# First operands of the last weights' products loaded and split inside the last gate and up block, residual loads placed later, the last form bank by bank

## The chip, the cores and the metric

The kernel runs on one core of one Trainium2 chip. The metric is the device time of one launch in microseconds, the median of several runs; before the change it was 1640.43 us (3 runs, 1640.39 to 1641.12). Engines: TensorE (PE, its weight loads PEld), VectorE (DVE), ScalarE (ACT), GpSimd (POOL) and SyncE (SP), which issues all transfers of the stage looked at here.

## The reference, cut to what matters

One decoder layer on 1024 tokens of width 1024: retention and differential attention side by side, a cross attention to 256 memory tokens, and a gated feed forward net with 2816 hidden columns. The change touches only the end:

```
h = rms_norm(x, norm_ffn[l])
x = x + (jax.nn.silu(h @ w_gate[l]) * (h @ w_up[l])) @ w_down[l]
```

All is float32.

## The kernel before, in words

**Float32 by halves.** Each operand is split into a high part (`sc.copy` on ScalarE rounds it to fp32r) and a low part (`low`, a subtraction on VectorE). `mm3` (line 131) makes a product of three matmuls: high with high, high with low, low with high.

**Gate and up** (lines 1187 to 1226). The hidden columns go in 22 blocks of 128, j = 0 to 21. Both matrix products of a block, gate and up, are done together by a scheme of seven products instead of eight: `Forms.form(f)` makes the seven sums or differences of weight quarters (f = 1, 2, 5, 6, 3, 7, 4) and splits them, `GU.prod(f)` is 12 matmuls (4 row blocks by 3) into one of three PSUM banks x, y, z, and `GU.after(f)` reads a bank when its sum is complete. The banks accumulate over several products, so a later product of the same bank waits until VectorE or ScalarE has read it. `after(7)` adds bank x into `U` on VectorE and then multiplies on GpSimd; `after(4)` multiplies on VectorE. The loop is rotated: in step j the last two products of block j (7 and 4) stand between the first five of block j + 1. In the last step, j = 21, there is no next block: products 7 and 4 stand alone with their reads between them.

**Down.** The product with `w_down` uses seven products as well. The seven forms of its left operand are made by `g_forms` (two blocks j make one pair p, 11 pairs) and stored in DRAM as `gF`; those of the weights by `w_forms`, stored in DRAM as `wT`; some quarters are used as they are. Then the loop in lines 1241 to 1265 goes over the forms f = 1, 2, 6, 5, 7, 3, 4 and, inside, over the pairs p = 0 to 10. Each (f, p) loads 128 x 512 of the left and 128 x 512 of the right operand (256 KB each, two issues on SP) into a stage tile `ds`, casts it (`dh`), subtracts (`dl`), and does 4 x 3 matmuls of 128 x 512 into four PSUM banks X or Y. After a form its four banks are added on VectorE to the residual tiles `res`, and finished quarters go to the output.

**Residual.** The eight tiles `res` (512 KB each) are loaded from DRAM, where an earlier stage has stored them. They lie in the four buffers of tag B (two tiles in each), which before hold the gate and up weights of the last two blocks (`gu`) and the two halves of form 4 of the activations (`B4`, read by product 4 of every block).

**Buffers.** Stage tiles of tag st (function `raw`): 3. Of tag t4: 6, used in the loop for `G`, for sums of weights, and for `gSa` and `gSb`, the sums of `g_forms`. Of tag xn (`xnp_tile`): 2, used for two of the weight sums. Split operands (tag w): 9, two for each (f, p).

**What sets the order.** A planner orders the instructions of each engine before the launch; on the chip every engine then goes through its list in that order, waiting on semaphores. An instruction issued while `pin[0]` is set stays behind everything that the program has traced on its engine before; this holds for the whole gate and up loop. TensorE's instructions always keep program order. Other instructions may move up to where the planner thinks them ready, which the loads of the down loop did.

Of the kernel before, what the change touches and what calls it, by code (L numbers as in the profile page):

```python
# [9 lines left out]
F32 = mybir.dt.float32  # L10
F32R = mybir.dt.float32r
# [5 lines left out]
P = 128  # L17
S = 1024
D = 1024
NT = 8  # L20
# [3 lines left out]
NH = HID // P  # L24
EPS = 1e-6
MAGIC = 0x5F3759DF
NP = NH // 2
# [3 lines left out]
U_RET, U_DIF, U_OUT, U_KV, U_XQ, U_XO, U_GU, U_DN = 0, 16, 28, 36, 52, 60, 68, 112  # L31
# [6 lines left out]
def body(ctx, tc, a, out):  # L38
# [18 lines left out]
    ve, sc, gp, sp = (Engine(e) for e in (nc.vector, nc.scalar, nc.gpsimd, nc.sync))  # L57
# [15 lines left out]
    up = ctx.enter_context(tc.tile_pool(name="up", bufs=NW))  # L73
# [8 lines left out]
    def t4(name, dt=F32):  # L82
        return tp4.tile([P, 1024], dt, tag="t4", name=name)
# [10 lines left out]
    def s2(name):  # L94
        return ps_s.tile([P, 1024], F32, tag="S", name=name)
# [8 lines left out]
    def low(eng, dst, src, hi):  # L104

        eng.tensor_tensor(out=dst, in0=src, in1=hi.bitcast(F32), op=ALU.subtract)

    def raw(name):
        return stp.tile([P, 1024], F32, tag="st", name=name)
# [21 lines left out]
    def mm3(ps, pairs, start=True, stop=True, **kw):  # L131

        n = len(pairs)
        for i, ((lh, ll), (rh, rl)) in enumerate(pairs):
            pe.matmul(ps, lh, rh, start=start and i == 0, stop=False, **kw)
            pe.matmul(ps, lh, rl, start=False, stop=False, **kw)
            pe.matmul(ps, ll, rh, start=False, stop=stop and i == n - 1, **kw)
# [631 lines left out]
    bp = p2.enter_context(tc.tile_pool(name="bp", bufs=1))  # L769
# [99 lines left out]
    res_d = [drp.tile([P, D], F32, tag=f"res{t}", name=f"res_d{t}") for t in range(NT)]  # L869
# [159 lines left out]
    def add(eng, dst, x, y):  # L1029
        eng.tensor_tensor(out=dst, in0=x, in1=y, op=ALU.add)  # L1030

    def sub(eng, dst, x, y):
        eng.tensor_tensor(out=dst, in0=x, in1=y, op=ALU.subtract)
# [39 lines left out]
    wd, wT = {}, {}  # L1073

    def w_load(p):
        wd[p] = [raw(f"wd{p}_{i}") for i in range(2)]
        for i in range(2):
            sp.dma_start(wd[p][i], a["w"][U_DN + 2 * p + i])

    def w_forms(p):  # L1080

        r = wd.pop(p)
        B11, B12, B21, B22 = r[0][:, 0:512], r[0][:, 512:1024], r[1][:, 0:512], r[1][:, 512:1024]
        sub(ve, B11, B12, B11)
        sub(ve, B12, B22, B12)
        sub(ve, B22, B22, B11)
        sub(ve, B21, B21, B22)
        wT[p] = drp.tile([2, P, 1024], F32, tag=f"wT{p}", name=f"wT_d{p}")
        for i in range(2):
            sp.dma_start(wT[p][i], r[i])  # L1090

    gF, Gs = {}, {}

    def g_forms(p):

        g1, g2 = Gs.pop(2 * p), Gs.pop(2 * p + 1)
        A11, A21, A12, A22 = g1[:, 0:512], g1[:, 512:1024], g2[:, 0:512], g2[:, 512:1024]
        x, y = t4(f"gSa{p}"), t4(f"gSb{p}")
        d = drp.tile([4, P, 1024], F32, tag=f"gF{p}", name=f"gF_d{p}")
        sp.dma_start(d[0][:, 0:512], A11)  # L1100
        sp.dma_start(d[1], g2)
        add(ve, x[:, 0:512], A21, A22)
        sub(ve, x[:, 512:1024], x[:, 0:512], A11)
        sub(ve, y[:, 0:512], A11, A21)
        sub(ve, y[:, 512:1024], A12, x[:, 512:1024])
        sp.dma_start(d[2], x)
        sp.dma_start(d[3], y)
        gF[p] = d

    class GU:  # L1110
# [37 lines left out]
        def go(self, f, c=slice(0, 512)):  # L1148
            self.prod(f, c)
            if f not in (1, 6):  # L1150
                self.after(f, c)

    c0, c1, call_ = slice(0, 256), slice(256, 512), slice(0, 512)
    f0 = Forms(0)
    f0.form(1, gp)
# [30 lines left out]
    pin[0] = True  # L1186
    for j in range(NH):
        n, c = None, c1 if j == 0 else call_
        if j % 2 == 0:
            w_load(j // 2)  # L1190
        if j + 1 < NH:
            n = GU(j + 1, fn)
            fm = Forms(j + 2) if j + 2 < NH else None
            n.prod(1)
            fn.form(5)
        o.prod(7, c)
        if n:
            fn.form(6)
            fn.form(3)
        o.after(7, c)  # L1200
        if n:
            n.prod(2)
            fn.form(7)
            n.after(2)
        o.prod(4, c)
        if n and fm:
            fm.form(1)
        o.after(4, c)
        if n:
            n.prod(5)  # L1210
            if fm:
                fm.form(2)
            n.after(5)
            n.prod(6)
            fn.form(4)
        if j % 2 == 0:
            w_forms(j // 2)
        if n:
            n.prod(3)
        if j % 2:  # L1220
            g_forms(j // 2)
        if n:
            n.after(3)
            fn = fm
        o = n
    pin[0] = False

    res = [bp.tile([P, 2, D], F32, tag="B", bufs=4, name=f"res{t}") for t in range(4)]
    res = [res[t // 2][:, t % 2] for t in range(NT)]
    for t in range(NT):  # L1230
        sp.dma_start(res[t], res_d[t])
    xs_ = [s2(f"dx{i}") for i in range(2)]
    X = [xs_[i // 2][:, 512 * (i % 2):512 * (i % 2) + 512] for i in range(4)]
    Y = [(mm, ms)[i // 2](f"dy{i}") for i in range(4)]
    gsrc = {1: (0, 0), 2: (1, 0), 4: (1, 1), 5: (2, 0), 6: (2, 1), 7: (3, 0), 3: (3, 1)}
    wsrc = {5: (0, 0), 7: (0, 1), 4: (1, 0), 6: (1, 1)}

    outs = {1: [(X, 0, 0)], 2: [(Y, 0, 0, 1)], 6: [(X, 0, 1)], 5: [(Y, 1, 1)], 7: [(X, 1, 1, 1)],
            3: [(Y, 0, 1, 1)], 4: [(X, 1, 0, 1)]}
    h5_ = lambda i: slice(512 * i, 512 * i + 512)  # L1240
    for f in (1, 2, 6, 5, 7, 3, 4):
        bank = Y if f in (2, 5, 3) else X
        for p in range(NP):
            s_ = raw(f"ds{f}_{p}")
            d, x = gsrc[f]
            sp.dma_start(s_[:, 0:512], gF[p][d][:, h5_(x)])
            if f in wsrc:
                d, x = wsrc[f]
                sp.dma_start(s_[:, 512:1024], wT[p][d][:, h5_(x)])
            else:  # L1250
                sp.dma_start(s_[:, 512:1024], a["w"][U_DN + 2 * p + (f > 1)][:, h5_(f == 3)])
            hi, lo = (up.tile([P, 1024], F32R, tag="w", name=f"d{x}{f}_{p}") for x in "hl")
            sc.copy(hi, s_)
            low(ve, lo, s_, hi)
            for i in range(4):
                sl = slice(P * i, P * i + P)
                mm3(bank[i], [((hi[:, sl], lo[:, sl]), (hi[:, 512:1024], lo[:, 512:1024]))],
                    start=p == 0 and f in (1, 2, 5), stop=p == NP - 1, skip_group_check=f not in (1, 2, 5))
        for b_, e, c, *last in outs[f]:
            for i in range(4):  # L1260
                t = 2 * i + e
                dst = res[t][:, h5_(c)]
                add(ve, dst, b_[i], dst)
                if last:
                    sp.dma_start(out[t][:, h5_(c)], dst)
    p2.close()


# [67 lines left out]
def build(arrays):  # L1336
    nc = bacc.Bacc("TRN2", target_bir_lowering=False, num_devices=1, dynamic_dma_scratch_size=1024)
    aps = {k: nc.dram_tensor(f"in_{k}_dram", v.shape, mybir.dt.from_np(v.dtype), kind="ExternalInput").ap()
           for k, v in arrays.items()}
    out = nc.dram_tensor("out_0_dram", (NT, P, D), F32, kind="ExternalOutput").ap()  # L1340
    with tile.TileContext(nc) as tc:
        with ExitStack() as ctx:
            body(ctx, tc, aps, out)
    return nc
# [10 lines left out]
```

## Time and profile before

| | |
|---|---|
| median of 3 runs | 1640.43 us |
| profiled execution, its own time | 1642.59 us |
| its span | 1640.8 us |
| TensorE busy | 1547.2 us, 94% |
| VectorE, ScalarE, GpSimd busy | 64%, 38%, 17% |
| chain that ended last | PE 75%, DVE 16%, ACT 3%, DMA 3% |
| mean granted TensorE clock | 0.982 |
| a residual load, a store of gF (gSa, gSb, second G), a store of wT | 512 KB |
| one operand pair of the down products | 2 x 256 KB |

Times are us from the start of the span. Busy shares are averages over all stages; what is read below is the stretch from the last gate and up block (from 1379 us) through the first down form (1417.7 to 1456.7) to the end. In a timeline row, the bracket at the end says how long the engine stood idle before the instruction and what released it. In a windows row the granted clock stands as a share of full speed (1.00 is 2.4 GHz, 0.50 is 1.2 GHz).

### The profile page before, as it was taken

What the parts mean: (1) busy time and instruction counts of PE and PEld (TensorE: products, weight loads), DVE (VectorE), ACT (ScalarE), POOL (GpSimd) and SP (SyncE); (2) the same over time, 40 slices, a digit from 0 to 9 for tenths busy, and PEclk for the clock granted to TensorE, in tenths of its full rate; (3) what the DMA queues carried; (4) which work ended last, traced back from release to release, by engine and by line L of the source; (5) the groups of instructions that cost most, each with busy time, mean ns of one, the idle gap of its engine ahead of it and who ended that gap; (6) DMA issues with size and microseconds to landing.
All of it is one profiled execution on the core that took longest, in us unless ns stands there. A gap on an engine that the chain in (4) does not pass through costs nothing.

```text
span 1640.8 us, 23170 instructions
## 1 busy us (share of the span) xinstructions
PE 1547.2 (94%) x8712; PEld 1321.6 (81%) x8712; DVE 1046.6 (64%) x2578; ACT 616.3 (38%) x1187; POOL 283.1 (17%) x238
## 2 busy tenths in 40 slices
PE   5899899999999989999999979999999999899998
PEld 5778878878877978799899858788888888688887
DVE  8864873873876543756666886666666666455554
ACT  4442442442444731333223353333333333243332
POOL 4323222222212331102112230010000000000000
PEclk9899999999999999999999989999999999999999
DMA  8201110110102562101101122444444444766564
GB/s 286 71 27 39 34 51 27 44 52 26 39 27 97 187 217 84 46 1 39 39 27 39 65 103 84 148 148 147 148 161 147 168 163 171 255 215 219 195 218 154
DMA packets 68079, 180.82 MB, mean 110 GB/s; under 512 B 7296, under 2 KB 12800, under 8 KB 67968
## 3 DMA queue, kind: packets, MB, share of 16 engines
q1 hardware_dynamic: 66960, 178.81, 30.8%
q8 instruction: 68, 1.11, 0.3%
q10 hardware_dynamic: 1008, 0.55, 0.1%
q14 instruction: 43, 0.35, 0.1%
HBM read 135.55 MB, written 43.78 MB: 109 GB/s over the span
## 4 chain that ended last, share of the span: by engine, by line
PE 75%; DVE 16%; ACT 3%; DMA 3%; issue 1%; POOL 1%; SPq 0%; ACTq 0%; DVEq 0%; POOLq 0%
PE x L64 14%; PE g_r L64 8%; PE z L64 7%; PE dx L64 7%; PE dy L64 5%; PE wo L64 5%; PE xo L64 5%; PE xq L64 4%; PE y L64 3%; PE kv L64 3%; PE q L64 2%; PE av L64 2%; DVE dsm L52 2%; DVE rw_d L52 2%; DVE nmx L52 1%
## 5 line engine op out<-in xcount | busy, mean ns | idle before, releaser
L64 PE MATMUL g_r<-uh_r,xT 128*128 128x512 f32 x512 | 178.2, 406 | 0.0
L52 DVE TENSOR_TENSOR dl<-ds,dh 128x1024 fp32r<-128x1024 f32 x77 | 94.2, 1224 | 98.0 <-PE dy L64 36.6
L52 ACT CAST dh<-ds 128x1024 fp32r<-128x1024 f32 x77 | 81.2, 1054 | 133.1 <-DMA ds<-in_w_dram 41.5
L64 PE MATMUL kv<-uh_d,xT 128*128 128x256 f32 x512 | 112.4, 302 | 6.2 <-DVE dql L52 6.2
L64 PE MATMUL x<-Bh,f 128*128 128x512 f32 (+1 forms) x368 | 114.6, 383 | 1.5 <-DVE G L52 1.4
L64 PEld LDWEIGHTS g_r<-uh_r,xT 128*128 128x128 f32 x512 | 96.4, 188 | 22.3 <-issue 2.5
L52 DVE TENSOR_TENSOR f<-s,f 128x512 fp32r<-128x512 f32 x86 | 65.0, 756 | 62.8 <-ACT f L52 62.8
L52 POOL TENSOR_TENSOR G<-G,U 128x512 f32<-128x512 f32 (+1 forms) x23 | 35.6, 1549 | 399.2 <-DVE U L52 381.3
L64 PE MATMUL g_r<-ul_r,xT 128*128 128x512 f32 x256 | 100.6, 393 | 0.0
L64 PEld LDWEIGHTS kv<-uh_d,xT 128*128 128x128 f32 x512 | 88.3, 200 | 8.7 <-DVE dql L52 6.4
L64 PE MATMUL xq<-hT,uh_xq 128*128 128x256 f32 x512 | 94.3, 286 | 0.0
L52 ACT CAST f<-s 128x512 fp32r<-128x512 f32 x88 | 54.6, 620 | 104.2 <-DVE s L52 102.5
L64 PE MATMUL xo<-uh_xo,xoT 128*128 128x512 f32 x256 | 90.2, 412 | 2.1 <-DVE B6l L52 1.6
L52 ACT ACTIVATE p<-s,nmx,dsm 128x128 f32<-128x128 f32 (+7 forms) x64 | 53.2, 832 | 98.6 <-DVE nmx L52 95.3
L64 PEld LDWEIGHTS x<-Bh,f 128*128 128x128 f32 x368 | 69.2, 191 | 15.2 <-DVE G L52 2.1
L64 PEld LDWEIGHTS xq<-hT,uh_xq 128*128 128x128 f32 x512 | 81.0, 195 | 0.0
L64 PE MATMUL kv<-ul_d,xT 128*128 128x256 f32 x256 | 74.8, 292 | 1.9 <-DVE ul_d L52 1.9
L52 DVE TENSOR_TENSOR f<-gu,f 128x512 fp32r<-128x512 f32 x63 | 43.4, 689 | 49.2 <-ACT f L52 49.2
L64 PE MATMUL dx<-dh 128*128 128x512 f32 x176 | 69.6, 396 | 5.2 <-ACT dh L52 5.2
L64 PE MATMUL xq<-hT,ul_xq 128*128 128x256 f32 x256 | 73.1, 286 | 0.0
L52 DVE TENSOR_TENSOR G<-x,G 128x512 f32<-128x512 f32 (+1 forms) x69 | 45.7, 662 | 41.9 <-ACT G L52 38.5
L64 PE MATMUL x<-Bl,f 128*128 128x512 f32 (+1 forms) x184 | 70.3, 382 | 0.0
(325 smaller groups left out, 4247.1 us busy)
## 6 DMA issues: line engine op xcount, KB each, us to landing
gu<-in_w_dram SPq DMA_DIRECT2D x21, 1024.0 KB, 6.0
ds<-gF_d SPq DMA_DIRECT2D x77, 256.0 KB, 2.9
wd<-in_w_dram SPq DMA_DIRECT2D x22, 512.0 KB, 5.6
wT_d<-wd SPq DMA_DIRECT2D x22, 512.0 KB, 3.0
ds<-wT_d SPq DMA_DIRECT2D x44, 256.0 KB, 3.4
ds<-in_w_dram SPq DMA_DIRECT2D x33, 256.0 KB, 3.3
st_r<-in_w_dram SPq DMA_DIRECT2D x16, 512.0 KB, 3.3
st_kv<-in_w_dram SPq DMA_DIRECT2D x16, 512.0 KB, 3.3
```

The source lines that it names most:

```text
L52: r = f(*args, **kw)
L64: return tc.keep_in_program_order(nc.tensor.matmul(*args, **kw))
```

## The change

A function `d_load` issues the two loads of a pair (f, p) into a given kind of tile, and `d_cast` casts and subtracts. In the last step of the gate and up loop, with the order pinned, the pairs p = 0, 1, 2 of form 1 are loaded at its start (into the two xn tiles and one stage tile) and split at three places: before `after(7)`, before `after(4)`, and at the end of the step behind `g_forms`. In the down loop the residual loads stand just before the pair p = 4 of the first form instead of before everything. Stage tiles alternate: odd pairs use tag st, even pairs tag t4. In the last form (f = 4) the products of the last three pairs are done bank by bank, each bank followed by its add and output.

```
+    def d_load(f, p, stage):
+        ds[f, p] = s_ = stage(f"ds{f}_{p}")
+        d, x = gsrc[f]
+        sp.dma_start(s_[:, 0:512], gF[p][d][:, h5_(x)])
...
+    def d_cast(f, p):
+        s_ = ds.pop((f, p))
+        hi, lo = du[f, p] = [up.tile([P, 1024], F32R, tag="w", name=f"d{x}{f}_{p}") for x in "hl"]
+        sc.copy(hi, s_)
+        low(ve, lo, s_, hi)
...
     for j in range(NH):
         n, c = None, c1 if j == 0 else call_
+        if j == NH - 1:
+            for p in range(3):
+                d_load(1, p, raw if p == 2 else xnp_tile)
...
+        else:
+            d_cast(1, 0)
         o.after(7, c)
...
         o.prod(4, c)
-        if n and fm:
+        if not n:
+            d_cast(1, 1)
+        elif fm:
             fm.form(1)
         o.after(4, c)
...
         if j % 2:
             g_forms(j // 2)
+        if not n:
+            d_cast(1, 2)
...
-    for t in range(NT):
-        sp.dma_start(res[t], res_d[t])
...
+    for f in d_order:
         for p in range(NP):
...
+            if f == d_order[0] and p == 4:
+                res2 = [bp.tile([P, 2, D], F32, tag="B", bufs=4, name=f"res{t}") for t in range(4)]
+                res = [res2[t // 2][:, t % 2] for t in range(NT)]
+                for t in range(NT):
+                    sp.dma_start(res[t], res_d[t])
+            if (f, p) not in du:
+                d_load(f, p, raw if p % 2 else t4)
+                d_cast(f, p)
+            if f != d_order[-1] or p < NP - 3:
+                for i in range(4):
+                    d_prod(f, p, i)
+        if f == d_order[-1]:
             for i in range(4):
+                for p in range(NP - 3, NP):
+                    d_prod(f, p, i)
+                d_out(f, i)
```

`d_prod(f, p, i)` is the `mm3` of bank i, `d_out(f, i)` the adds and outputs of bank i, both as they stood in the loop.

## Rows read from the trace of the kernel before

**Rows 1.** The chain of waits that ended last: start us, us, what

```profile
1414.04 0.70 DVE U L52
...
1414.88 3.00 PE x L64 x12
...
1417.88 5.47 PE dx L64 x24
...
1425.31 7.50 DMA ds<-in_w_dram
...
1432.91 1.05 ACT dh L52
...
1433.99 1.23 DVE dl L52
...
1435.27 21.41 PE dx L64 x83
...
1636.23 0.69 DVE res L52
```

**Rows 2.** Timeline of TensorE: start us, us, engine, instruction, idle time before

```profile
954.44 0.63 PE L68 MATMUL bt<-ident,bs 128*128 128x128 f32 x4 [2.63 <-DVE ry_f L52]
...
1413.61 0.39 PE L64 MATMUL x<-Bh,f 128*128 128x512 f32 x1
...
1434.01 0.79 PE L64 MATMUL dx<-dh 128*128 128x512 f32 x1 [5.17 <-ACT dh L52]
```

**Rows 3.** Windows: length us, PE busy (instructions), granted clock, DMA share, GB/s

```profile
955.00:955.75 0.75, 0.72 (x5) 0.80 0.00 0
...
958.75:959.50 0.75, 0.75 (x8) 0.92 0.00 0
...
1433.00:1433.50 0.50, 0.00 (x0) 0.82 0.84 324
...
1440.00:1440.50 0.50, 0.50 (x3) 0.85 1.03 295
```

**Rows 4.** Timeline of the SP queue: start us, us of issuing, transfer

```profile
1386.50 0.32 SPq L52 DMA_DIRECT2D res<-res_d  x1
...
1389.40 1.82 SPq L52 DMA_DIRECT2D wd<-in_w_dram  x2
...
1391.26 0.45 SPq L52 DMA_DIRECT2D res<-res_d  x1
...
1391.76 0.48 SPq L52 DMA_DIRECT2D ds<-gF_d  x1
...
1406.00 0.79 SPq L52 DMA_DIRECT2D res<-res_d  x2
...
1417.68 0.32 SPq L52 DMA_DIRECT2D res<-res_d  x1
...
1422.17 0.32 SPq L52 DMA_DIRECT2D gF_d<-gSb  x1
...
1422.54 2.20 SPq L52 DMA_DIRECT2D res<-res_d  x3
...
1424.84 0.42 SPq L52 DMA_DIRECT2D ds<-gF_d  x1
```

**Rows 5.** Timeline of VectorE: start us, us, engine, instruction, idle time before

```profile
1405.29 0.69 DVE L52 TENSOR_TENSOR f<-gu,f 128x512 fp32r<-128x512 f32 x1 [3.27 <-ACT f L52]
...
1419.12 1.22 DVE L52 TENSOR_TENSOR dl<-ds,dh 128x1024 fp32r<-128x1024 f32 x1
...
1634.87 2.65 DVE L52 TENSOR_TENSOR res<-dx,res 128x512 f32<-128x512 f32 x4 [8.24 <-PE dx L64]
```

**Rows 6.** DMA rate from 1390 to 1440 us in 40 slices

```profile
GB/s 403 256 302 328 403 392 113 13 0 0 0 0 0 56 387 380 413 390 197 329 402 375 243 300 328 374 410 275 383 252 397 365 323 398 324 48 21 252 138 192
```

**Rows 7.** Timeline of ScalarE: start us, us, engine, instruction, idle time before

```profile
1416.52 1.05 ACT L52 CAST dh<-ds 128x1024 fp32r<-128x1024 f32 x1 [4.92 <-DMA ds<-in_w_dram]
```

**Rows 8.** The output transfers: duration ns min/median/max, first and last start us

```profile
L52 SPq DMA_DIRECT2D out_dram<-res x16: 332/338/430, 1485.8 to 1637.5; - x16
```

More of the change, by code (lines that the diff above doesn't have):

```diff
@@ L1151, in go @@
                 self.after(f, c)
+    gsrc = {1: (0, 0), 2: (1, 0), 4: (1, 1), 5: (2, 0), 6: (2, 1), 7: (3, 0), 3: (3, 1)}
+    wsrc = {5: (0, 0), 7: (0, 1), 4: (1, 0), 6: (1, 1)}
+    d_order = (1, 2, 6, 5, 7, 3, 4)
+    ds, du = {}, {}
+    h5_ = lambda i: slice(512 * i, 512 * i + 512)
+    def d_load(f, p, stage):
+        ds[f, p] = s_ = stage(f"ds{f}_{p}")
+        d, x = gsrc[f]
+        sp.dma_start(s_[:, 0:512], gF[p][d][:, h5_(x)])
+        if f in wsrc:
+            d, x = wsrc[f]
+            sp.dma_start(s_[:, 512:1024], wT[p][d][:, h5_(x)])
+        else:
+            sp.dma_start(s_[:, 512:1024], a["w"][U_DN + 2 * p + (f > 1)][:, h5_(f == 3)])
+    def d_cast(f, p):
[3 more added lines that the diff above has]
+        low(ve, lo, s_, hi)
     c0, c1, call_ = slice(0, 256), slice(256, 512), slice(0, 512)
@@ L1199, in body @@
             fn.form(3)
+        else:
+            d_cast(1, 0)
         o.after(7, c)
@@ L1226, in body @@
     pin[0] = False
-    res = [bp.tile([P, 2, D], F32, tag="B", bufs=4, name=f"res{t}") for t in range(4)]
-    res = [res[t // 2][:, t % 2] for t in range(NT)]
-    for t in range(NT):
-        sp.dma_start(res[t], res_d[t])
+    res = []
     xs_ = [s2(f"dx{i}") for i in range(2)]
@@ L1234, in body, with d_prod @@
     Y = [(mm, ms)[i // 2](f"dy{i}") for i in range(4)]
-    gsrc = {1: (0, 0), 2: (1, 0), 4: (1, 1), 5: (2, 0), 6: (2, 1), 7: (3, 0), 3: (3, 1)}
-    wsrc = {5: (0, 0), 7: (0, 1), 4: (1, 0), 6: (1, 1)}
     outs = {1: [(X, 0, 0)], 2: [(Y, 0, 0, 1)], 6: [(X, 0, 1)], 5: [(Y, 1, 1)], 7: [(X, 1, 1, 1)],
             3: [(Y, 0, 1, 1)], 4: [(X, 1, 0, 1)]}
-    h5_ = lambda i: slice(512 * i, 512 * i + 512)
-    for f in (1, 2, 6, 5, 7, 3, 4):
-        bank = Y if f in (2, 5, 3) else X
-        for p in range(NP):
[L1244 to L1254, printed above, removed]
+    def d_prod(f, p, i):
+        hi, lo = du[f, p]
+        sl = slice(P * i, P * i + P)
+        mm3((Y if f in (2, 5, 3) else X)[i], [((hi[:, sl], lo[:, sl]), (hi[:, 512:1024], lo[:, 512:1024]))],
+            start=p == 0 and f in (1, 2, 5), stop=p == NP - 1, skip_group_check=f not in (1, 2, 5))
@@ new lines, in d_out @@
+    def d_out(f, i):
+        for b_, e, c, *last in outs[f]:
+            t = 2 * i + e
+            dst = res[t][:, h5_(c)]
+            add(ve, dst, b_[i], dst)
+            if last:
+                sp.dma_start(out[t][:, h5_(c)], dst)
+    for f in d_order:
+        for p in range(NP):
+            if f == d_order[0] and p == 4:
[10 more added lines that the diff above has]
+        if f == d_order[-1]:
@@ L1255, in body @@
             for i in range(4):
[L1256 to L1259, printed above, removed]
+                for p in range(NP - 3, NP):
+                    d_prod(f, p, i)
+                d_out(f, i)
+        else:
             for i in range(4):
[L1261 to L1265, printed above, removed]
+                d_out(f, i)
```

## The prediction, made before the change was run

> **What bounds the kernel now.** I read the chain of waits first, over its last 240 us [rows 1]. Up to 1409 us it is TensorE alone, block after block; from 1435.27 us on it is TensorE alone again. Between them it leaves TensorE three times. Twice VectorE must read a PSUM bank before the next product may add to it; the second time it is the add into U (0.70 us), which ends 0.14 us before the last gate/up product starts at 1414.88. Then the first form of the down products begins and runs out of operands: a load (7.50 us of DMA), a cast on ScalarE (1.05) and the subtraction on VectorE (1.23) stand in the chain before TensorE goes on. That is the fifth operand pair, p = 4: 4 pairs of 12 products each were ready, the fifth was not.
>
> The timeline of TensorE shows the price [rows 2]: 5.17 us of idle time before the product at 1434.01, then a wait for the low part until 1435.27 [rows 1]. The windows with the granted clock show the second half of it [rows 3]: the clock falls from full to 0.5 (from 2.4 to 1.2 GHz) in the window at 1433.0 and is full again only in the window at 1440.0. Altogether: 7 forms x 132 products at 29.92/132 = 0.227 us would take 209.4 us from 1417.7; they took until 1636.2, so 9.0 us are lost, all in this form. The two waits for VectorE's reads of a bank are short beside that.
>
> Why is p = 4 late? The issue order of the SP queue tells it [rows 4]. Once the last gate/up product has ended (1417.88), SP issues one residual load, three stores of gF, three more residual loads (2.20 us of issuing), and only at 1424.84 the load of p = 4. The bytes in between are seven transfers of 512 KB; with p = 4's own 512 KB, 4.19 MB. It was cast at 1432.91.
>
> **Two rules of order, read from the same rows.** The planner gives buffers of one tag away in program order: of the three stage buffers two held the weights loaded at 1389.40, the third had been free for the whole loop, and yet the first down load came at 1391.76, right after them. Among what is ready it takes what stands earlier in the program: weights (1389.40) before the second residual load (1391.26) that had been ready since 1386.50, and that before the down load. I assume that both rules hold in the changed kernel.
>
> **The change, part by part.**
>
> *First pair, loaded inside the last block.* The loads of p = 0 to 2 are pinned on SP behind the two stores of wT. Those wait for four subtractions after the split of the last form at 1405.29 [rows 5]; with pitches of 0.6 us the first store goes at 1407.2, the second at 1408.4, the load of p = 0 at 1408.9 to 1409.3. (Before, it was issued at 1391.76 and its data lay there in time. So this edit makes it 17 us later.) Ahead of it in the queue: the residual load of 1406.00 and both stores. Whether one or two residual loads go ahead is a choice: the same pattern one block earlier (a buffer free, two VectorE operations, a store) let one residual load through at 1386.50 and the next only at 1391.26, behind what stood earlier in the program [rows 4]. I take one: 4 x 0.524 = 2.10 MB. The DMA rate by slices of 1.25 us [rows 6] is 56 GB/s to 1407.5 and then 387, 380, 413, 390: 2.03 MB by 1412.5, so 2.10 MB at 1412.7. From bytes to cast is 1.0 us: the first load behind the stores (2.88 MB by the same sum, reached at 1415.5) let the cast start at 1416.52 [rows 7]. So p = 0 can be cast at 1413.7.
>
> Here lies a new wait. The cast and the subtraction of p = 0 are pinned ahead of the add into U. Behind the cast on ScalarE nothing urgent queues; behind the subtraction on VectorE queues the add into U, and for that TensorE waits. 1413.7 + 1.05 + 1.23 + 0.70 + 0.14 and 0.05 of gaps = 1416.85 against 1414.88: **+2.0 us** (with two residual loads ahead +3.3; if the load were early, 0).
>
> *Its clock.* TensorE then idles from 1414.0 (the last matmul before, at 1413.61, and its 0.39) [rows 2] to 1416.85, 2.9 us. The nearest row is the idle time of 2.63 us before 954.44 [rows 2]: the clock was down from about 955.2 to 958.9 [rows 3], some 3.5 us at half speed, which cost 1.7 us. I take **+1.7**; bounds 0 and 3.3 (the 6.7 us of low clock after the 5.17 us, halved). The product starts at 1416.85, so most of it falls inside it, and its end moves from 1417.88 to 1421.6.
>
> *p = 1, 2, 3.* Loads of p = 1 and 2 follow at 1.35 us each (0.524 MB at 0.39), their casts are done before TensorE asks for them at 2.7 us apart; the subtraction of p = 2 stands behind the last multiplication and the four form sums (0.7 + 4 x 0.6 us after the product's end) and is ready 4.4 us after it, needed after 5.4. p = 3 takes the buffer of the first stored weight. No cost: bounds 0 and 1, hidden by what comes next. The store of gF's first quarter moves behind six issues; its reader is p = 10 of this form, 27 us later.
>
> *Residual loads later; p = 4 in a t4 buffer.* Residual loads now stand in the program behind p = 3, still ahead of p = 4. Four of them need the two buffers of B4, free when the last product ends, as at 1417.68. And p = 4 now takes a t4 buffer: by the first rule not before gSb of the last block has its own, which is the third of the four form sums after that product. By then four residual loads are ready and stand earlier. So the order of rows 4 repeats: residual, three stores, three residuals, p = 4. **The stall stays.** What changes is a little: the subtraction of 1.22 us that lay between the form sums at 1419.12 [rows 5] is ahead of the product now, so gSb's store and all behind it go 1.2 us earlier. Before, from the product's end to p = 4's second product: 1435.27 - 1417.88 = 17.4. I take 17.4 - 1.2 = 16.2. Upper end 17.4 (as before). Lower end 15.3: 4.19 MB at 390 GB/s, the best sustained rate of rows 6, 10.75 us, plus 1.2 from issue to first bytes, 1.0, 1.05, 1.23 and 0.1 of gaps. So p = 4's second product starts at 1421.6 + 16.2 = 1437.8, **+2.5** against 1435.27, in which the +2.0, +1.7 and -1.2 are contained.
>
> What the rate is worth: between 1418.75 and 1431.0 the slices give 342 GB/s. The Trainium skill (DMA: Bandwidth & Descriptors, Specifications) states about 358 GB/s as the HBM limit of a core; by that these 4.19 MB would take 11.7 us, an estimate, in place of 12.3, and the sum would be 0.6 us lower. The trace's slices of 413 GB/s lie above that limit, so I go by the slices.
>
> *Clock after p = 4.* Idle 1421.6 + 10.9 = 1432.5 to 1436.5, 4.0 us, against 5.17: same fall, 0. Lower bound -2.4 (12 products at 0.427 in place of 0.227, if it stayed up).
>
> *Forms 2 to 7.* Nine stage buffers in place of three. TensorE has no idle time there (the chain is TensorE without a break from 1435.27 on), so nothing to gain: 0.
>
> *Last form bank by bank.* The last three pairs run bank after bank, so banks end 9 products (2.0 us) apart instead of 3 (0.7). Before, four adds of 0.69 on VectorE queue from 1634.87 on for 2.65 us [rows 5], and the last output is issued at 1637.5 [rows 8]; the last product had released VectorE at 1636.23 [rows 1]. The last add can start then, some 0.6 us sooner than as fourth in that queue: **-0.6**. Bounds 0 and -1.2 (an emptier DMA queue). Pairs 8 to 10 must be split before bank 0 ends; the last subtraction was done 8.24 us before 1634.87, at 1626.6; TensorE asks for it at 1636.2 less 30 products of 0.227, 1629.4: covered by 2.8 us.
>
> **Sum.** +2.5 + 0 - 0.6 = +1.9 us on the profiled execution (span 1640.8, its time 1642.59, 2.2 us above the median of the runs). Taken to the median 1640.43: **1642.3**, I write 1642. Own range: 1639.5 to 1644.5, from +3.3 for two residual loads, the clock's 0 to 3.3, and 15.3 to 17.4.
>
> **The rivals.**
> *A residual load more in front of the first pair* (slower). Place: the SP queue at 1406. Both residual loads went there before (the row of 1406.00 has x2) [rows 4]. Then p = 0 lands at 1415.0, U is 3.3 us late, TensorE idles 4.2 us and the low clock costs up to 3.3 as after the 5.17 us: 1.9 + 1.3 + 1.6 = +4.8, 1645.2. It decides from a landing later than about 1414.5. Against: the pattern of 1386.50.
> *p = 4 goes ahead of the residual loads.* Then the 9.0 us go, the late U stays (+3.7), the tail gives 0.6: -5.9, 1634.5. For: that the loads are in another place in the program. Against: both rules of order.
> *All covers hold*, first pair in time too: -9.0 - 0.6 = -9.6, 1630.8. Against: the issue at 1409 behind 2 MB.
> *The change does next to nothing*: U in time, p = 4 as late as before: -1.2 - 0.6 = -1.8, 1638.6. It would take a landing by 1411.7.
>
> **How the numbers follow.** Forecast 0.58, one more residual load 0.15, p = 4 early 0.15, all covers 0.06, next to nothing 0.06. What can be told from no change here is 0.2%, 3.3 us: below 1637.1 faster, above 1643.7 slower. Faster: 0.15 + 0.06 + 0.03 (a forecast with every bound low) = 0.24. Slower: 0.14 of the second case and 0.06 of the forecast's upper end = 0.20. Same 0.56. The range reaches down to the p = 4 case and up to the second: 1634 to 1645.5.
>
> **What would show it.** Right: the first gate/up product after U starts about 1416.9, VectorE's add into U waiting for the subtraction of dl; in the SP queue p = 4 behind four residual loads; an idle time of 3 to 5 us in the first down form again, with a clock of 0.5 behind it; the last add alone. Wrong: the first down form without idle time, p = 4 issued before the residual loads, or the last gate/up product starting at 1414.9 as before.

## The result and the profile after

The changed kernel takes 1650.26 us (median of 5 runs, 1646.46 to 1652.14) against 1640.39 us before (5 runs on the same chip, 1637.25 to 1641.12): ratio 1.0062, interval [1.0045, 1.008]. It is slower, and 8.3 us above the forecast of 1642.0. Two more measurements gave 1.0044 [1.003, 1.0059] and 1.0038 [1.0024, 1.0051].

The profiled execution has a span of 1650.3 us, 9.5 us more than before. Not all of it belongs to the change. ScalarE reads bank z into G once in every gate and up block. The first and the last of these reads, in the trace of before and then in that of after:

```profile
985.28 0.37 ACT L52 COPY G<-z 128x256 f32<-128x256 f32 x1 [1.78 <-PE z L64]
...
1409.62 0.59 ACT L52 COPY G<-z 128x512 f32<-128x512 f32 x1 [3.42 <-PE z L64]
```

```profile
989.85 0.37 ACT L52 COPY G<-z 128x256 f32<-128x256 f32 x1 [1.77 <-PE z L64]
...
1413.97 0.59 ACT L52 COPY G<-z 128x512 f32<-128x512 f32 x1 [4.37 <-PE z L64]
```

Up to the last read TensorE does the same work in both kernels; only some loads and one cast lie elsewhere. The 4.4 us by which it comes later after the change are there at the first read already (4.6), behind stages that the change does not touch. In sixteen traces of twelve kernels the first read started anywhere from 980.3 to 989.9 us and the last from 1404.4 to 1414.0 (the kernel before at 1409.62 and 1409.18, the changed one at 1413.97, 1407.66 and 1409.53), while the time between the two was 424.0 to 425.1 us in all of them. So I count **local time** from the last read on. The kernel before ends at local 231.2, the changed one at 236.3: the change costs 5.2 us in its own stretch.

The chain of waits that ended last, after the change (start us, us, what), answers to [rows 1]:

```profile
1414.00 5.21 DMA ds<-in_w_dram
...
1419.31 1.05 ACT dh L52
...
1420.39 0.59 DVE dl L52
...
1421.53 0.70 DVE U L52
...
1422.36 5.46 PE x L64 x12
1427.82 5.53 PE dx L64 x24
...
1434.62 6.55 DMA ds<-in_w_dram
...
1443.68 21.27 PE dx L64 x83
...
1638.39 0.70 DVE res L52
...
1639.14 4.41 PE dx L64 x18
...
1643.57 0.70 DVE res L52
...
1644.32 2.38 PE dx L64 x9
```

Three places are to be seen. First, a new chain ahead of the last gate and up product: load, cast, subtraction, and only then the add into U, so the product starts at local 8.39 (before 5.26) and takes 5.46 us in place of 3.00. Second, the fifth pair's load still stands in the chain: its second product comes at local 29.71 (before 25.65). Third, in the last form the chain leaves TensorE twice for an add of 0.70 us, which it did not before [rows 1, 5]; against that the end comes 3.6 us after the last matmul in place of 4.6. VectorE's first three adds of that form:

```profile
1638.39 0.69 DVE L52 TENSOR_TENSOR res<-dx,res 128x512 f32<-128x512 f32 x1 [3.48 <-PE dx L64]
1641.53 0.69 DVE L52 TENSOR_TENSOR res<-dx,res 128x512 f32<-128x512 f32 x1 [2.44 <-PE dx L64]
1643.57 0.69 DVE L52 TENSOR_TENSOR res<-dx,res 128x512 f32<-128x512 f32 x1 [1.35 <-PE dx L64]
```

TensorE stops for the add of bank 0 before it starts on bank 1, and for that of bank 2 before bank 3. Between banks 1 and 2 it does not stop: the adds are 3.1 us apart where it stops and 2.0 where it does not.

TensorE's waits from 1410 us to the end, largest first (engine and line, what it waited for: us in total, times, longest):

```profile
PE x L64 <- DVE U L52: 4.0, 1, 4.0
PE dx L64 <- ACT dh L52: 3.6, 1, 3.6
PE dx L64 <- DVE res L52: 1.6, 2, 0.8
...
```

The SP queue after, in the columns of [rows 4]:

```profile
1395.77 14.90 SPq L52 DMA_DIRECT2D res<-res_d  x2
1411.67 1.77 SPq L52 DMA_DIRECT2D wT_d<-wd  x2
1413.54 0.41 SPq L52 DMA_DIRECT2D ds<-gF_d  x1
...
1427.43 0.32 SPq L52 DMA_DIRECT2D res<-res_d  x1
...
1431.11 0.32 SPq L52 DMA_DIRECT2D gF_d<-gSb  x1
1431.48 2.56 SPq L52 DMA_DIRECT2D res<-res_d  x3
1434.09 0.48 SPq L52 DMA_DIRECT2D ds<-gF_d  x1
```

This is the order that the prediction read off: one residual load (the second of the two in the first row, issued at 1410.35), both stores of wT, the first pair, and later residual, three stores, three residuals, p = 4.

The windows around the last gate and up product, with more columns than [rows 3] (length us; busy us and instructions of PE, PEld, DVE, ACT, POOL; granted clock, DMA share, GB/s):

```profile
1420.00:1421.00 1.00, 0.00 (x0) 0.00 (x0) 0.61 (x1) 0.36 (x1) 0.00 (x0) 0.99 0.88 301
1421.00:1422.00 1.00, 0.00 (x0) 0.00 (x0) 1.00 (x2) 0.99 (x1) 0.00 (x0) 0.50 0.94 338
...
1426.00:1427.00 1.00, 1.00 (x4) 0.81 (x3) 0.00 (x0) 0.00 (x0) 0.00 (x0) 0.50 0.01 2
1427.00:1428.00 1.00, 1.00 (x4) 0.77 (x4) 0.14 (x1) 0.00 (x0) 0.00 (x0) 0.60 0.00 0
1428.00:1429.00 1.00, 1.00 (x6) 0.82 (x5) 1.00 (x2) 0.00 (x0) 0.00 (x0) 1.00 0.51 143
```

TensorE stood idle from 1418.3 to 1422.4; the granted clock fell to 0.50 (1.2 GHz) inside this time and came back at 1427.8, as the product ended. The second idle time, 3.65 us in front of p = 4, was followed by a low clock again: 83 matmuls took 21.27 us, where 83 x 0.227 would be 18.8.

### The profile page after: what moved, and what is told of

Its sections match the earlier page's. It is cut to its first block, busy times and chain, and to the rows that moved or that the text cites. A ratio compares the mean times of both kernels' runs of the same rounds, so it can differ in the third digit from the quotient of the medians.

```text
span 1650.3 us, 23147 instructions
## 1 busy us (share of the span) xinstructions
PE 1555.4 (94%) x8712; PEld 1327.6 (80%) x8712; DVE 1046.7 (63%) x2578; ACT 616.7 (37%) x1187; POOL 283.1 (17%) x238
## 4 chain that ended last, share of the span: by engine, by line
PE 75%; DVE 16%; DMA 3%; ACT 3%; issue 1%; POOL 1%; SPq 0%; ACTq 0%; POOLq 0%
PE x L64 14%; PE g_r L64 8%; PE z L64 7%; PE dx L64 7%; PE dy L64 5%; PE wo L64 5%; PE xo L64 5%; PE xq L64 4%; PE y L64 3%; PE kv L64 3%; PE q L64 2%; PE av L64 2%; DVE dsm L52 2%; DVE rw_d L52 1%; DVE nmx L52 1%
```

## The experiments

The theory: three places, each with its own cause (a late first pair, residual loads ahead of p = 4, two banks in one tile). Against it stood rivals that are named where they apply. The table gives local times in us, so that the earlier stages are left out, and beside it the timed ratio to the kernel before on the same chip. "Fifth pair" is the start of its second product, "second form" the start of the first product of f = 2.

| kernel | last gate/up product | fifth pair | second form | end | end against before | ratio, interval |
|---|---|---|---|---|---|---|
| before | 5.26 | 25.65 | 47.05 | 231.2 | 0 | 1 |
| e6_before | 5.25 | 25.44 | 47.05 | 231.2 | 0.0 | 1.0002 [0.9992, 1.0012] |
| after | 8.39 | 29.71 | 50.99 | 236.3 | +5.2 | 1.0062 [1.0045, 1.008] |
| e0_after | 8.82 | 29.85 | 51.30 | 236.6 | +5.4 | 1.0044 [1.003, 1.0059] |
| e12_after | 9.42 | 30.83 | 51.98 | 237.3 | +6.1 | 1.0038 [1.0024, 1.0051] |
| e1_order | 5.26 | 27.13 | 48.26 | 233.5 | +2.4 | 1.0013 [1.0, 1.0026] |
| e10_loads | 5.26 | 24.88 | 46.76 | 232.1 | +0.9 | 1.0007 [0.9992, 1.0021] |
| e11_fill | 8.67 | 28.93 | 50.75 | 236.0 | +4.9 | 1.0039 [1.0024, 1.0055] |
| e2_res | 8.35 | 24.73 | 43.88 | 229.2 | -2.0 | 1.0011 [0.9998, 1.0025] |
| e14_res | 9.48 | 26.45 | 45.56 | 230.9 | -0.3 | 1.0 [0.9989, 1.0011] |
| e7_before_res | 5.25 | 21.49 | 40.59 | 225.5 | -5.6 | 0.9974 [0.9963, 0.9985] |
| e3_tail | 8.92 | 30.26 | 51.59 | 235.4 | +4.3 | 1.0026 [1.0013, 1.0039] |
| e4_banks | 8.50 | 29.41 | 51.25 | 234.4 | +3.2 | 1.0018 [1.0009, 1.0027] |
| e5_all | 5.26 | 21.67 | 40.79 | 223.9 | -7.3 | 0.9955 [0.9939, 0.9971] |
| e9_stage | 7.91 | no wait | 40.84 | 225.1 | -6.0 | 0.9956 [0.9942, 0.9971] |
| e13_early_all | 5.25 | 20.47 | 39.58 | 222.7 | -8.5 | 0.9958 [0.9944, 0.9971] |

**The two kernels once more.** e0_after and e12_after are the changed kernel, e6_before the one before, unchanged.

> The changed kernel once more, unaltered, as the reference of the runs beside it. Its first trace had three places that cost more than before: the last gate/up product (+5.6 us by its end, of which 3.1 the wait and 2.5 the low clock), the last form (+2.2), less 1.0 at the very end, less 1.6 up to the fifth pair's second product: +5.1 us after 1380 us; and 4.4 us before 1380 us, in code that the change does not touch. Theory 'three places': the 4.4 us are a low clock in the output projection that falls in some runs and not in others, so this run gives 1645 to 1652 with the same +5.1 after the start of the last block. Rival 'earlier stages': the 4 us before the last block belong to the change and show again in this trace and in every kernel built on it.

> The kernel before, unaltered, for a second trace and as a measure of what two sets of runs of one kernel differ by. Theory 'three places': from the read of the last z bank (1409.6 in the first trace) to the end it takes 231.2 us again, within 0.5, against 236.3 and 236.6 in two traces of the changed kernel; what differs between runs lies before that read. Rival 'earlier stages': the read comes at 1407 or earlier in most runs of this kernel, as it does in the later traces of the changed one, and the stretch behind it varies by several us too, so that part of the measured 7 to 10 us lies elsewhere. Time: ratio 1.000 within 0.0015.

> The changed kernel once more, as it is. Three places: from ScalarE's last read of z the same within 0.5 us as in its two traces so far: last gate/up product at 8.4 to 8.9 and 5.3 to 5.5 us long, fifth pair's second product at 29.7 to 29.9, end at 236.3 to 236.7. Rival earlier stages: the time over the kernel before is again over 7 us, while the local part is 5.2 to 5.5, and the rest stands ahead of the last block and differs from trace to trace.

The local part of the kernel before is the same within 0.1 us; that of the changed kernel varies, 236.3 to 237.3, with the moment at which the first pair lands. In e12_after it was later than expected (8.4 to 8.9): the load in front of the cast took 6.12 us in place of 5.21, and the product started at 9.42. The rival of earlier stages did not hold: in e0_after ScalarE's last read of z comes at 1407.66 us, sooner than in either trace of the kernel before.

**The late first pair.** e1_order splits the first pair behind `after(7)` in place of ahead of it; e10_loads keeps that order and puts the three pinned loads one step of the loop earlier, behind form 7 of the last block.

```
# e1_order
-        else:
-            d_cast(1, 0)
         o.after(7, c)
+        if not n:
+            d_cast(1, 0)
# e10_loads
-        if j == NH - 1:                    # at the start of the step
...
+        if j == NH - 2:                    # behind n.after(2)
+            for p in range(3):
+                d_load(1, p, raw if p == 2 else xnp_tile)
```

> The split of the first pair stands behind the add into U in place of ahead of it; all else as in the changed kernel. Theory 'late pair': the last gate/up product starts 0.9 us after the one before it again and runs at full clock, its end is 5.6 us sooner; the fifth pair is still late (residual loads ahead of it), its second product 15.5 to 16.5 us behind that end; 4.5 to 5.6 us faster than the changed kernel. Rival 'memory traffic': the bytes in the queue, not the order on VectorE, hold everything; then the fifth pair lands at the same time as in the changed kernel and less than 2 us come back. A second rival: the first pair now holds the first down product by itself, since its data lands about 1415 and must be split before 1417.7; then up to 1 us remains there.

> The changed kernel with the three pinned loads one step of the gate/up loop earlier (behind form 7 of the last block, ahead of both stores of wT). Three places: with the data there in time the first pair's split is done before the add into U needs VectorE, so the last gate/up product starts at 5.3 after ScalarE's last read of z and takes 3.0 us at full clock (changed kernel 8.4 to 8.8, and 5.3 to 5.5 us long); the fifth pair stays late, 15.5 to 16.5 us after that product's end; local end 5 us below the changed kernel's, 231 to 232. Rival: the order by itself costs (the cast and subtraction pinned ahead of U), however early the data are: start at 7.5 or later, local end 234 to 237.

The chain of e10_loads (start us, us, what):

```profile
1407.78 0.59 ACT G L52
...
1412.20 0.70 DVE U L52
...
1413.04 3.00 PE x L64 x12
1416.04 5.47 PE dx L64 x24
...
1423.06 7.14 DMA ds<-in_w_dram
...
1432.66 1.65 PE dx L64 x3
```

With the data there in time, the same pinned order costs nothing: the product starts at 5.26 at full clock, and the local end falls 4.2 to 5.2 us below that of the changed kernel. So the wait needs both, a late landing and a cast pinned ahead of the add: with early data the place of the cast costs nothing here, and with the cast behind the add (e1_order) the late landing does not reach the product. p = 4 came 16.62 us after the product's end, just above the expected 15.5 to 16.5. In e1_order the product is on time as well, but the subtraction of the second pair now stands ahead of the last multiplication, the stores follow later, and all four residual loads go in a row before p = 4:

```profile
1420.50 2.35 SPq L52 DMA_DIRECT2D res<-res_d  x4
1422.90 0.47 SPq L52 DMA_DIRECT2D ds<-gF_d  x1
```

Its fifth pair came 18.9 us after the product's end, not the expected 15.5 to 16.5, so against the kernel before 1.5 us are lost at the next place.

**The clock by itself.** e11_fill puts 18 matmuls that nothing reads between the last two gate and up products, so TensorE is not idle while it waits for U.

```
         o.after(7, c)
+        if not n:
+            fill = mm("fill")
+            A_, (bl, bh) = o.fs[7], b_tiles(7)
+            for i in range(18):
+                pe.matmul(fill, A_[:, 0, 0:P], bh[:, i % 4, :], start=i == 0, stop=i == 17)
```

> The changed kernel with 18 extra matmuls of form operands into a bank of their own that nothing reads, between the last two gate/up products, so that TensorE isn't idle while U is late. Low clock from the idle time: the product still starts late, at 8.4 to 9 after ScalarE's last read of z, but takes 3.0 us in place of 5.46, so the fifth pair and the end come 2.0 to 2.5 us earlier: local end 234 to 234.7. Rival, the low clock has another reason (an earlier stage, or the wait for VectorE at the bank itself): the product takes 5 us or more again, and the end doesn't move, 236.3 to 236.6.

Its timeline of TensorE, a window beside it, and its chain:

```profile
1416.50 4.24 PE L64 MATMUL fill<-Bh,f 128*128 128x512 f32 x18
```

```profile
1423.00:1424.00 1.00, 1.00 (x6) 0.81 (x5) 0.01 (x1) 1.00 (x1) 0.10 (x1) 1.00 1.03 404
```

```profile
1420.95 3.00 PE x L64 x12
1423.95 5.50 PE dx L64 x24
...
1430.79 7.96 DMA ds<-in_w_dram
...
1441.21 4.21 PE dx L64 x9
```

Half of the expectation held: without the idle time the product takes 3.00 us at clock 1.00, so the low clock did come from the idle time. The other half did not: the fifth pair follows 20.26 us after the product's start, against 21.32 in the profile after, 21.03 in e0_after and 21.41 in e12_after. Of 2.46 us of product only 0.8 to 1.1 arrive there. The load of p = 4 takes 7.96 us in place of 6.55. In the windows of the changed kernel the transfers had run dry at the end of the slow product (2 and 0 GB/s from 1426 to 1428), while here they still move 404 GB/s in its last microsecond. My reading is that what TensorE gains, p = 4 loses by starting behind a DMA that has not caught up. Other traces agree: the load of p = 4 takes 6.3 to 6.8 us in the four whose product takes about 5.46 us (after, e0_after, e12_after, e3_tail), 7.07 in e4_banks with a product of 4.31, and 7.96 here with 3.00. No run tried the DMA by itself.

What an idle time costs is not fixed, either. TensorE is idle for 4.0 us ahead of the product in the profile after, for 4.0 in e2_res and 4.1 in e4_banks; the product takes 5.46 us in the first and 4.3 in the other two, since the clock was back at 1.00 sooner there.

**The residual loads.** e2_res and e14_res move them from in front of p = 4 to behind the last pair of the first form; e7_before_res does this in the kernel before.

```
-            if f == d_order[0] and p == 4:
+            if f == d_order[0] and p == NP - 1:     # now behind d_load and d_cast
                 res2 = [...]
```

> The residual loads stand in the program behind the last pair of the first down form; all else as in the changed kernel. Theory 'residuals ahead': three of the four residual loads that went ahead of the fifth pair go behind it, so its bytes fall from 4.19 to 2.6 MB, it can be multiplied about 12 us after the end of the last gate/up product in place of 15.9, TensorE idles under 1.5 us there and the clock stays up: 5 to 6.5 us faster than the changed kernel. Rival 'buffer': the fifth pair's t4 buffer, given only after the form sums, is what makes it late; then it comes as late as before and nothing changes.

> The changed kernel with the residual loads behind the last pair of the first form, as traced once before. Earlier stages: its part behind ScalarE's last read of z is again 229 to 229.5 us, 2 us below the kernel before, and the time over the kernel before is whatever the stages ahead of it add, -2 to +2. Rival buffer or memory traffic in the last block: in this trace the fifth pair or a later one of the first form is late (second form from 46 on, local end 231 or later), which would explain the +1.8 timed.

> The kernel before with one part of the change alone, placed further down: the residual loads stand in the program behind the last pair of the first down form, everything else as before. Theory 'residuals ahead': one residual load and three stores stay ahead of the fifth pair, three residual loads go behind it; its bytes are 2.6 MB, it is ready about 11.2 us after the last gate/up product in place of 17.4, needed after 10.9; idle time under 1 us, no low clock: 8 us faster than before (7 to 9). Rival 'memory traffic': the residual loads only move and hit a later pair; then 0 to 3 us faster.

The SP queue of e2_res:

```profile
1423.03 0.32 SPq L52 DMA_DIRECT2D gF_d<-gSb  x1
1423.40 0.44 SPq L52 DMA_DIRECT2D ds<-gF_d  x1
...
1431.48 1.67 SPq L52 DMA_DIRECT2D res<-res_d  x3
```

p = 4 now goes right behind the stores. Its load takes 5.0 to 5.5 us in the chains of these kernels, and TensorE waits for it 0.5 to 1.8 us in place of 3.7 to 5.6. In the kernel before this one move is worth 5.6 us locally and 0.9974 timed, less than the 7 to 9 us expected: the second form starts 6.5 us sooner, but the end comes 5.4 us behind the last matmul in place of 4.6; why is not settled. So most of the stall was the residual loads' doing. e2_res had been timed 3.8 us above what its trace said; its profiled execution, 1638.30 us, was the shortest of its twelve (median 1643.9). The second trace (e14_res) has the first pair landing later again (product at 9.48), a local end 1.7 us later, and a timed ratio of 1.0. So part of it does lie in the last block, through the first pair, as neither theory had put it.

**The last form.** e3_tail puts it back to pair by pair; e4_banks keeps it bank by bank, but in the order 0, 2, 1, 3.

```
# e3_tail
-            if f != d_order[-1] or p < NP - 3:
-                for i in range(4):
-                    d_prod(f, p, i)
-        if f == d_order[-1]:
...
+            for i in range(4):
+                d_prod(f, p, i)
+        for i in range(4):
+            d_out(f, i)
# e4_banks
-            for i in range(4):
+            for i in (0, 2, 1, 3):
                 for p in range(NP - 3, NP):
                     d_prod(f, p, i)
                 d_out(f, i)
```

> The last form pair by pair as before the change; all else as in the changed kernel. Theory 'shared tile': TensorE waited twice 0.8 us in the last form because two PSUM banks lie in one tile and the add of one holds the product into the other; without it the last form takes 29.9 us again in place of 32.1, and the last adds queue again (+1.0): 1.2 us faster than the changed kernel (0.5 to 2). Rival: the products bank by bank cost TensorE time in themselves or the order saves at the end as meant; then 0 to 1 us slower.

> The last form bank by bank in the order 0, 2, 1, 3, so that two neighbouring steps use different tiles of two banks; all else as in the changed kernel. Theory 'shared tile': both waits of TensorE for the add go, the last form takes 29.9 to 30.2 us in place of 32.1, and the end keeps its 1.0: 2 us faster than the changed kernel. Rival 'VectorE': the add itself, not the shared tile, holds TensorE; then the waits stay, two of 0.8 us, and the time does not change.

The end of the chain of e4_banks:

```profile
1607.54 29.93 PE dx L64 x132
...
1637.49 0.69 DVE res L52
```

Both remove the two waits (29.93 us for the 132 matmuls in place of 32.1 with the waits); e4_banks keeps the short end too (3.6 us behind the last matmul; e3_tail 4.3). The four banks X are halves of two tiles, `xs_[i // 2]`: bank 1 may not be written while VectorE reads bank 0, because they are one tile. With the neighbour in the other tile the same add lies beside the matmuls. The Trainium skill (PSUM — Partial Sum Buffer, section "PSUM bank collisions raise a hardware error") forbids two engines the same bank, not two banks; by that the wait is the kernel's own bookkeeping by tile, and e4_banks agrees as far as it goes: TensorE fills a bank while VectorE reads another, with no wait. Writing one half of a tile while the other is read was not tried.

**All repairs together.** e5_all has the edits of e1_order, e2_res and e4_banks; e13_early_all those of e10_loads, e2_res and e4_banks; e9_stage is the kernel before with the residual loads behind, the bank order 0, 2, 1, 3 and the pairs 1 and 2 staged in the two xn tiles.

> Three repairs in the changed kernel at once: the split of the first pair behind the add into U, residual loads behind the last pair of the first form, the last form in the order of banks 0, 2, 1, 3. Theory 'three places': they act in different stretches and nearly add up: no late U and no low clock there (-4.4 after the repair of the residual loads, of which 1 to 2 come back because the fifth pair then is needed sooner than it can come), the fifth pair in time within 1 to 3 us, no waits in the last form: 5 to 8 us faster than the kernel before, 10 to 13 faster than the changed one. Rival 'earlier stages': 4 us lie before the last block, so that it ends within 3 us of the kernel before.

> The kernel before with three edits: pairs 1 and 2 of the first down form are staged in xn tiles (their loads may go out early, pinned to nothing), the residual loads stand behind the last pair of the form, the last form's last three pairs run bank by bank in the order 0, 2, 1, 3. All times are from ScalarE's read of the last z bank. Late pair and residuals ahead: more pairs in hand before the last gate/up product ends, and no 512 KB transfers ahead of the rest, so the first down form runs without an idle time: its second form starts at 38.0 to 39.6 (before 47.05, with the residual loads behind alone 40.59), local end 221 to 223 against 231.2 before. Rival VectorE: the subtractions of pairs 1 and 2 now stand on VectorE between those of the form sums, delay the multiplication or the sum that the stored gF quarters wait for, and TensorE stands still in another pair: second form from 41 on, local end 224 or later.

> The changed kernel with all three places repaired: the pinned loads one step of the loop earlier, the residual loads behind the last pair of the first form, the last form's banks in the order 0, 2, 1, 3. Times from ScalarE's last read of z. Three places are all there is: last gate/up product at 5.3, 3.0 us long, first down form without an idle time (second form at 38.0 to 38.5), last six forms 179.5, tail 3.6 to 4.7; local end 221 to 222.7, 8.5 to 10 below the kernel before, and a timed ratio of 0.9935 to 0.9955. Rival, another stall comes forward (operands of pairs 3 to 6 behind the stores of wT and gF on the same DMA engines): second form from 39 on, local end 223 or later, no better than the repair by the order of the casts (223.9).

The chain of e13_early_all, and that of e9_stage:

```profile
1414.14 3.01 PE x L64 x12
...
1421.86 5.03 DMA ds<-in_w_dram
...
1429.36 19.11 PE dx L64 x83
```

```profile
1413.63 4.22 PE x L64 x12
...
1418.72 3.00 PE x L64 x12
1421.71 29.93 PE dx L64 x132
```

All three beat both kernels, and the times do not tell them apart (0.9955 to 0.9958). e9_stage has no idle time in the first form at all, but its two subtractions stand between those of the weight sums and delay the add ahead of product 7, much as its rival said: product 7 waits 2.9 us in place of 1.4 and takes 4.22 us in place of 3.03, from about 1415 us on at a granted clock of 0.50, so that the last gate and up product comes at 7.91 and the local end at 225.1 in place of the expected 221 to 223. e13_early_all is locally the shortest, 8.5 us below before; it still loses 1.4 us in front of p = 4, whose load goes out only behind the three stores, so its second form starts at 39.58, where its rival and not the theory had put it.

## Why the prediction was wrong, point by point

**What held.** Both rules of order, and with them the whole SP queue: the first pair behind the stores of wT with one residual load ahead of it, p = 4 behind four residual loads. The new wait of TensorE for U through the first pair's subtraction. The stall of p = 4: 15.86 us from the end of the gate and up product to its second product, 16.2 predicted. That the number fits is in part luck: the load of p = 4 goes out 0.7 us sooner behind that end than before, not 1.2, and takes 6.55 us in place of 7.50; in e11_fill, with the product at full clock, the stall is 17.26. The low clock behind p = 4: 83 matmuls take 21.27 us, before 21.41. Nothing in forms 2 to 7: from the second form to the last matmul 179.5 us in every kernel whose last form is free of waits.

**The term that failed in sign: the last form bank by bank.** The prediction gave it -0.6. It was +2.2 for two stops of 1.1 us (0.33 until the last matmul is through: 18 matmuls take 4.41 us, not 18 x 0.227; and 0.77 for the add), less 1.0 at the end, +1.2 in all. I had worked out when the operands and the last add are ready, and never asked what shares a tile with the bank that VectorE reads; the line `xs_[i // 2]` stood in the code, and it needed only that each of the four adds be set against the next bank's first matmul. e4_banks shows what the term could have been: the last form without a wait, and -1.0 at the end.

**The term that was mis-sized: the first pair and its clock.** Predicted: castable at 1413.7, U late by 2.0, the product's end late by 3.7. Measured, taken to the time of before: cast at 1414.96, U late by 3.1 (3.6 and 4.2 in the other two traces), the product's end late by 5.6. The issue was where it was expected (1409.2 in before's time, 1408.9 to 1409.3 predicted). The step that failed is the rate: I had put 2.10 MB, the first pair's 0.52 MB among them, at some 390 GB/s, the slices of [rows 6] up to 1412.5. The same slices of 1.25 us from 1400 us on in the profile after:

```profile
GB/s 364 30 0 13 0 0 0 0 0 269 370 413 249 215 302 295 298 380 413 419 152 0 66 364 377 403 360 213 308 357 418 383 390 377 400 393 390 400 365 388
```

From 1411.25 on, 2.10 MB are through at 1418.2, 302 GB/s on the mean. [rows 6] had the same fall: 197 GB/s in the slice from 1412.5 on, behind those that I used. There too the loads of operand pairs follow the stores of wT (issued from 1408.34 on, the pairs from 1410.78), while the faster slices ahead of it carried the two residual loads and the stores. So the rate for the pair was taken from other transfers. Why the slices fall there, to 215 after the change, is open. The rival with one residual load more put the limit of the landing at 1414.5 and the price at +4.8; its price was near, its cause was not what happened. The clock I had read from the idle time of 2.63 us as +1.7 (by the mean of 0.80 in [rows 3] it fell there at about 955.45, not 955.2, which leaves the 3.5 us as they are); the idle time grew to 4.0 us and the whole product ran at half speed, +2.46. But by e11_fill only 0.8 to 1.1 of that reach p = 4. So the fifth pair is late by 4.1 to 5.2 against the +2.5 of the sum.

**The sum in local time.** Predicted +2.5 - 0.6 = +1.9; measured +4.1 at p = 4, -0.1 up to the second form, +2.2 and -1.0 in the last form: +5.2.

**What the local time does not hold.** Timed first, the change cost 9.9 us; the two later measurements put it near 7 and 6 us, with local parts of 5.4 and 6.1. Over all kernels of the table the timed difference lies within 2 us of the local one, but for e2_res (3.8 us above) and this first measurement (4.7 above). In its trace the excess is there at the first read of z, and the profiled execution, 1652.14 us, was the longest of the five; where it comes from is not settled. That the change costs more than its stretch shows is not shown. Of the chances on record, the 0.20 for slower was the one that came.

**With the causes known.** e13_early_all is the change with its three places repaired, and takes 0.9958 of the time before. Of its 8.5 us of local gain, 5.6 stand in e7_before_res too, which only moves the residual loads. Of the other 2.8, 1.8 lie behind the last matmul (3.6 us in place of 5.4) and 1.0 in the first form. The timed intervals of the two kernels overlap, so what splitting the first operands early is worth by itself is not shown.

## What to carry to other kernels

Operands that are to be split in an earlier stage must also be loaded ahead of that stage's stores, or be split behind what TensorE waits for; else the wait moves to a busier place. Here the same pinned order cost 3 to 4 us of lateness with loads at local -0.4 and nothing with loads a step earlier. Before a loop is turned bank by bank, look which banks share a tile. And look first for what stands in a queue without being urgent: moving eight residual loads behind the form gained, alone, more than half of what all the edits together did.

## What the runs showed of the hardware that was not expected

A product at half clock cost less than its longer time in front of a load: 2.46 us longer, 0.8 to 1.1 us later at the next load's product, while the transfers ran dry meanwhile (2 GB/s against 404). The granted clock fell 2.6 us after TensorE's last matmul and stayed at 0.50 until 5.4 us of unbroken matmuls had run; after nearly the same idle time (4.1 us, e4_banks) the product took 4.31 us and not 5.46, so one idle time with its price is no table for the next. Both kernels' DMA rate fell, to 197 and 215 GB/s, where loads of operand pairs followed stores to DRAM, from slices of about 390 and 413 just ahead. And the start of the same stage moves by up to 6.3 us between executions of one kernel, more than the change is worth in its own stretch; only an instruction that both kernels have, taken as zero, made the traces comparable.
